# Sending x through DRAM on another queue, with later takes and a longer last part of the down projection

## The chip, the cores and the metric

The kernel runs on one core of one Trainium2 chip. The metric is the device time of one execution in microseconds. TensorE is PE in what follows, VectorE DVE, ScalarE ACT, GpSimd POOL and SyncE SP; PEld is PE's loading of weights.

## The reference

The reference is a decoder trunk of four layers over x, 256 rows of 1024 floats. Each layer is three blocks: a SwiGLU feed-forward (inner width 2816) with half weight, a mixer, and a second SwiGLU. The mixer is a short gated convolution in layers 0 and 3, latent attention in layer 1 and chunked spatial gating in layer 2.

```python
def swiglu(x, w_gate, w_up, w_down):
    return (jax.nn.silu(x @ w_gate) * (x @ w_up)) @ w_down

for i in range(DEPTH):
    x = x + 0.5 * swiglu(rms_norm(x, norm_g[i, 0]), ffn_gate[i, 0], ffn_up[i, 0], ffn_down[i, 0])
    hn = rms_norm(x, norm_g[i, 1])
    x = x + mixer(hn)                     # conv, latent attention or spatial gating, by i % 3
    x = x + 0.5 * swiglu(rms_norm(x, norm_g[i, 2]), ffn_gate[i, 1], ffn_up[i, 1], ffn_down[i, 1])
```

All is float32, and all weights are read once from DRAM.

## The kernel before

x stays in SBUF as two tiles of 128 rows (x0 and x1). Each has its own stream of work, a Python generator; stream 0 is four turns ahead of stream 1, and after that the two take turns. Both use the same weights, each unit of them once.

Weights come in units of 128 x 1024 floats: two k-tiles of 512 columns, or one k-tile of 1024. `W.load` (L91) issues a unit's DMA on SP into one of 6 raw buffers. `W.make` writes whi, the unit rounded for the fast matmul, on ACT (L104), and `W.complete` wlo, the rest, on DVE (L111); there are 9 pairs of these. A raw buffer's next load is issued right behind the wlo that frees it. Activations are split in the same way (L244 on ACT, L245 on DVE), and each product is three matmuls (L290, L291, L293). So one turn of one stream, with one unit, is six matmuls of 128 x 512.

The order on every engine is written out by hand. `later(n, fn)` puts work off by n turns, counted over both streams; `later(1, ..)` runs at the end of the same turn.

A block ends in `rows_into_x`: the first k-tiles go into both column halves of the result, and the last `tail` k-tiles first into half 0 and then into half 1. The end of a half adds it to x (`residual`, L391 after a feed-forward, L389 after a mixer) and calls `prepare_x`, which makes the left operand of the next block: x transposed, scaled by the norm's gain, split in two. Some halves are transposed by PE (`turn_by_pe`, L252 and L430). The others go through DRAM: a transpose within 32 x 32 squares on DVE (L406), a write to DRAM (L411), four reads (L415), and a "take" of four scalings on ACT (L420) and the split (L244, L245). Writes and reads stand on ACT's own DMA queue. X_WRITE, X_READ and X_TAKE say how many turns after the half's end they come. Both halves go through DRAM after a feed-forward, except ahead of the attention, where half 1 goes by PE; after a mixer half 0 goes by PE. Each stream does 17 such round trips, 34 in all.

```python
DOWN_TAIL, OUT_TAIL = 8, 4
X_TURN, X_WRITE, X_READ, X_TAKE = 2, 1, 4, 8
```

DOWN_TAIL is the tail of the down projection (22 k-tiles), OUT_TAIL that of a mixer's last product (8). The square sum of x for the norm (L372) stands on ACT. The feed-forward's hidden tiles go through DRAM too (`turned`), with write (L266) and reads (L270) on SP. While a stream is between blocks, weights are made 3 units ahead, else 4 (`CHAIN_AHEAD`, `AHEAD`).

Of the kernel before, what the change touches and what calls it, by code (L numbers as in the profile page):

```python
# [47 lines left out]
AHEAD = 4  # L48
CHAIN_AHEAD = 3
LAG = 4  # L50
DOWN_TAIL, OUT_TAIL = 8, 4
X_TURN, X_WRITE, X_READ, X_TAKE = 2, 1, 4, 8
IDLE_FIRST, IDLE_DMA, IDLE_PE, IDLE_MLA = 1, 2, 2, 4
SKEW = 2
K_POOL, K_SUM, K_SCALE, K_TURN, Q_ROPE, Q_TURN, Q_SUM, Q_WAIT = 2, 2, 3, 2, 1, 3, 3, 3
# [10 lines left out]
class Weights:  # L66


    def __init__(self, nc, raw_pool, pool):
        self.nc, self.raw_pool, self.pool = nc, raw_pool, pool  # L70
        self.raws = []
        self.units = []
        self.made = []
        self.half_made = []
        self.loaded = []

    def add(self, w, c0, width, n_kt, per_unit, k=0):

        v = w.rearrange("(kt p) n -> p kt n", p=P)
        while k < n_kt:  # L80
            n_rows = min(n_kt - k, per_unit * (1 if len(self.units) < SMALL else max(1, PER_RAW * UNIT // (per_unit * width))))
            for j in range(0, n_rows, per_unit):
                self.units.append((len(self.raws), j, min(per_unit, n_rows - j), width))
            self.raws.append((v[:, k : k + n_rows, c0 : c0 + width], n_rows, width))
            k += n_rows
# [23 lines left out]
    def complete(self):  # L109
        for hi, lo, src, upto in self.half_made:  # L110
            self.nc.vector.tensor_tensor(out=lo, in0=src, in1=hi.bitcast(F32), op=ALU.subtract)  # L111
            self.load(upto)
        self.half_made.clear()

    def get(self, u, ahead):
        for _ in range(2):
            if len(self.made) < min(len(self.units), u + ahead):
                self.make()
        return self.made[u]
# [3 lines left out]
def trunk(ctx: ExitStack, tc: tile.TileContext, x, positions, norm_g, ffn_gate, ffn_up, ffn_down,  # L123
          conv_w_in, conv_k, conv_w_out, mla_w_a, mla_q_norm, mla_w_uq, mla_kv_norm, mla_w_ukv,
          mla_q_gain, mla_k_gain, mla_w_o, sg_w_in, sg_v_norm, sg_w_s, sg_b, sg_w_out, out):
    nc = tc.nc
# [12 lines left out]
    def name(tag):  # L139
        ids[0] += 1  # L140
        return f"{tag}_{ids[0]}"

    def slot(shape, dtype=F32):
        return slots.tile(shape, dtype, tag="s", name=name("s"))
# [20 lines left out]
    def later(turns, fn):  # L165
        ids[0] += 1
        put_off.append((turn[0] + turns, ids[0], fn))
# [8 lines left out]
    W = Weights(nc, raw_pool, w_pool)  # L176
# [64 lines left out]
    def split(src, shape):  # L241

        hi, lo = slot(shape, F32R), slot(shape, F32R)
        nc.scalar.activation(hi, src, AF.Copy)  # L244
        nc.vector.tensor_tensor(out=lo, in0=src, in1=hi.bitcast(F32), op=ALU.subtract)  # L245
        return hi, lo
# [128 lines left out]
    def square_x(t, h):  # L375
        sums_of_x[t][h] = square_sum(x_half(t, h))
# [6 lines left out]
    def x_half(t, h):  # L383
        return xs[t][:, h * 512 : (h + 1) * 512]
# [8 lines left out]
    def gain_at(i, which, h):  # L393
        g0 = (i * 3 + which) * NK + 4 * h
        return columns[0][:, g0 : g0 + 4]

    def prepare_x(t, h, i, which, halves_by_dma):

        g = gain_at(i, which, h)
        lhs[t][h] = None  # L400
        later(1, lambda: square_x(t, h))
        if not halves_by_dma[h]:
            later(X_TURN, lambda: turn_by_pe(t, h, g))
            return
        z = slot([P, 4, 4, 32])
        nc.vector.transpose(z.rearrange("p j k b -> p k j b"), x_half(t, h).rearrange("p (k j b) -> p k j b", j=4, b=32))  # L406
        d = dram.tile([4, 32, 4, 4, 32], F32, tag="xturn", name=name("xturn"))
        y = slot([P, 4, 4, 32])

        def write():  # L410
            nc.scalar.dma_start(out=d.rearrange("i a j k b -> (i a) j k b"), in_=z)  # L411

        def read():
            for j in range(4):
                nc.scalar.dma_start(out=y[32 * j : 32 * j + 32], in_=d[:, :, j].rearrange("i a k b -> a i k b"))  # L415

        def take():
            xg = slot([P, 4, P])
            for k in range(4):
                nc.scalar.activation(xg[:, k, :].rearrange("p (i b) -> p i b", b=32), y[:, :, k], AF.Copy, scale=g[:, k : k + 1])  # L420
            lhs[t][h] = split(xg, [P, 4, P])

        later(X_WRITE, write)
        later(X_READ, read)
        later(X_TAKE, take)

    def turn_by_pe(t, h, g):
        tr = transposed([xs[t][:, (4 * h + k) * P : (4 * h + k + 1) * P] for k in range(4)])
        xg = slot([P, 4, P])
        nc.vector.tensor_tensor(out=xg, in0=tr, op=ALU.mult, in1=g.unsqueeze(2).broadcast_to([P, 4, P]))  # L430
        lhs[t][h] = split(xg, [P, 4, P])
# [593 lines left out]
```

## Time and profile before

| | |
|---|---|
| median of 3 runs | 1918.91 us (1911.62 to 1919.62) |
| the profiled execution's own time | 1915.99 us |
| its span | 1914.3 us |
| PE busy | 1861.1 us, 97% of the span |
| DVE, ACT busy | 1121.0 us, 917.8 us |
| mean granted clock of PE | 0.990 |
| DMA | 209 GB/s over the span |

Busy time of PE is the time in which at least one matmul was under way; matmuls overlap, so the mean of one (385 ns) is longer than the time from one start to the next. Engines that are not busy may still be held: ACT's time at issuing DMAs, and at waiting in its queue for one that has not landed, is not counted as busy.

### The profile page before, as it was taken

To read this page: it belongs to the slowest core of one execution; us is meant where nothing else is said; L and a number is where in the kernel's file an instruction comes from. 1 tells how busy PE (TensorE), PEld (TensorE's weight loads), DVE (VectorE), ACT (ScalarE), POOL (GpSimd) and SP (SyncE) were. 2 spreads that over 40 slices of the span, in tenths; PEclk is the share of its full clock that TensorE was granted. 3 is DMA by queue.
4 is the path that set the end of the run, shared out by engine and by line. 5 is a ranking of instruction groups with operands and counts; after the bars stand their busy time and mean duration, and the time that the engine had idled before them with its cause. 6 is when DMAs were issued, how large, how long until landed. Compare 5 with 4: busy or idle time off the path is not lost.

```text
span 1914.3 us, 23335 instructions
## 1 busy us (share of the span) xinstructions
PE 1861.1 (97%) x8518; PEld 1514.9 (79%) x8518; DVE 1121.0 (59%) x1357; ACT 917.8 (48%) x1300; POOL 104.7 (5%) x222
## 2 busy tenths in 40 slices
PE   9999999999999989999989999999999999999999
PEld 7888777888688868788868887878887887787887
DVE  5564575665566466666456655655646564766562
ACT  5443545443544376544454445454435443545442
POOL 1000000000421031000010000000000000000000
PEclk9999999999999988999999999999999999999999
DMA  7776556776677630677768776567866785566782
GB/s 259 246 234 215 187 180 196 243 240 211 202 247 238 201 118 23 196 239 235 231 188 260 231 234 184 175 204 240 256 204 206 238 263 186 178 195 196 239 252 94
DMA packets 224883, 400.25 MB, mean 209 GB/s; under 512 B 17126, under 2 KB 77696, under 8 KB 224768
## 3 DMA queue, kind: packets, MB, share of 16 engines
q1 hardware_dynamic: 199280, 379.25, 62.9%
q10 hardware_dynamic: 24880, 18.41, 3.2%
q0 software_dynamic: 608, 1.11, 0.3%
q8 instruction: 66, 1.08, 0.2%
q14 instruction: 49, 0.40, 0.1%
HBM read 365.67 MB, written 33.03 MB: 208 GB/s over the span
## 4 chain that ended last, share of the span: by engine, by line
PE 80%; DMA 7%; ACT 6%; DVE 4%; ACTq 2%; issue 1%; DVEq 0%
PE acc L291 26%; PE acc L293 26%; PE acc L290 25%; DMA s<-xturn 4%; DMA xturn<-s 3%; DVE wlo L111 2%; ACT whi L104 2%; ACTq L415 2%; PE tr L252 1%; ACT s L372 1%; ACT s L420 1%; PE acc L927 1%; ACT s L244 1%; PE acc L900 1%; DVE x L391 1%
## 5 line engine op out<-in xcount | busy, mean ns | idle before, releaser
L290 PE MATMUL acc<-whi,s 128*128 128x512 f32 (+1 forms) x2664 | 1032.1, 387 | 15.9 <-ACT whi L104 14.1
L291 PE MATMUL acc<-wlo,s 128*128 128x512 f32 (+1 forms) x2664 | 1026.2, 385 | 17.5 <-DVE wlo L111 17.4
L293 PE MATMUL acc<-whi,s 128*128 128x512 f32 (+1 forms) x2664 | 983.5, 385 | 0.0
L111 DVE TENSOR_TENSOR wlo<-raw,whi 128x1024 fp32r<-128x1024 f32 (+1 forms) x634 | 750.8, 1213 | 250.8 <-ACT whi L104 245.7
L104 ACT ACTIVATE whi<-raw 128x1024 fp32r<-128x1024 f32 (+1 forms) x634 | 639.0, 1048 | 262.3 <-PE acc L293 140.9
L290 PEld LDWEIGHTS acc<-whi,s 128*128 128x128 f32 x2664 | 504.0, 189 | 130.5 <-ACT whi L104 23.5
L291 PEld LDWEIGHTS acc<-wlo,s 128*128 128x128 f32 x2664 | 503.8, 189 | 129.2 <-DVE wlo L111 25.9
L293 PEld LDWEIGHTS acc<-whi,s 128*128 128x128 f32 x2664 | 503.2, 189 | 107.0 <-DVE s L245 2.3
L468 ACT ACTIVATE s<-acc,rstd 128x512 f32<-128x512 f32 (+1 forms) x96 | 62.6, 652 | 434.8 <-PE acc L293 428.8
L476 DVE SCALAR_TENSOR_TENSOR s<-acc,rstd,s 128x512 f32<-128x512 f32 (+1 forms) x96 | 67.6, 704 | 186.1 <-PE acc L293 184.5
L277 DVE TENSOR_TENSOR s<-big,s 128x512 fp32r<-128x512 f32 x96 | 61.7, 643 | 128.0 <-ACT s L276 128.0
L380 POOL TENSOR_TENSOR total<-ss,ss 128x1 f32<-128x1 f32 x26 | 17.3, 664 | 1475.0 <-ACT s L372 1475.0
L245 DVE TENSOR_TENSOR s<-s,s 128x512 fp32r<-128x512 f32 (+1 forms) x58 | 39.5, 681 | 63.6 <-ACT s L244 63.6
L372 ACT ACTIVATE s<-x 128x512 bf16<-128x512 f32 x48 | 30.0, 625 | 90.6 <-DVE x L391 51.5
L276 ACT ACTIVATE s<-big 128x512 fp32r<-128x512 f32 x96 | 56.2, 586 | 27.8 <-DMA big<-turn 27.5
L391 DVE SCALAR_TENSOR_TENSOR x<-acc,x 128x512 f32<-128x512 f32 x32 | 22.0, 688 | 78.6 <-PE acc L293 78.6
L478 DVE STREAM_TRANSPOSE big<-s 128x512 f32<-128x512 f32 (+1 forms) x96 | 64.1, 667 | 3.3
L244 ACT ACTIVATE s<-s 128x512 fp32r<-128x512 f32 (+1 forms) x58 | 36.4, 627 | 41.7 <-DVE s L526 21.6
L420 ACT ACTIVATE s<-s,columns 128x128 f32<-128x128 f32 x136 | 43.2, 388 | 27.5 <-DMA s<-xturn 27.4
L252 PE MATMUL tr<-ident,s 128*128 128x128 f32 (+1 forms) x222 | 34.5, 284 | 8.1 <-DVE s L770 3.3
L252 PEld LDWEIGHTS tr<-ident,s 128*128 128x128 f32 (+1 forms) x222 | 26.7, 141 | 16.0 <-DVE s L770 5.1
L406 DVE STREAM_TRANSPOSE s<-x 128x512 f32<-128x512 f32 x34 | 24.2, 712 | 1.2
(123 smaller groups left out, 414.6 us busy)
## 6 DMA issues: line engine op xcount, KB each, us to landing
raw<-in_ffn_gate_dram SPq DMA_DIRECT2D x176, 512.0 KB, 4.8
raw<-in_ffn_up_dram SPq DMA_DIRECT2D x176, 512.0 KB, 4.8
raw<-in_ffn_down_dram SPq DMA_DIRECT2D x176, 512.0 KB, 4.9
raw<-in_conv_w_in_dram SPq DMA_DIRECT2D x48, 512.0 KB, 4.3
turn<-big SPq DMA_DIRECT2D x32, 512.0 KB, 4.2
big<-turn SPq DMA_DIRECT2D x128, 128.0 KB, 4.1
xturn<-s ACTq DMA_DIRECT2D x34, 256.0 KB, 2.5
s<-xturn ACTq DMA_DIRECT2D x136, 64.0 KB, 3.7
```

Of the source, the lines that this page charges most:

```text
L104: nc.scalar.activation(hi, src, AF.Copy)
L111: self.nc.vector.tensor_tensor(out=lo, in0=src, in1=hi.bitcast(F32), op=ALU.subtract)
L252: nc.tensor.transpose(tr[: part.shape[-1], n, :], part, ident)
L276: nc.scalar.activation(hi.rearrange("p k (i b) -> p k i b", b=32), src, AF.Copy)
L277: nc.vector.tensor_tensor(out=lo.rearrange("p k (i b) -> p k i b", b=32), in0=src, in1=hi.bitcast(F32).rearrange("p k (i b) -> p k i b", b ...
L290: nc.tensor.matmul(ps, lhsT=ah[:, k, :], rhs=wh[:, wk, c], start=first, stop=False)
L291: nc.tensor.matmul(ps, lhsT=ah[:, k, :], rhs=wl[:, wk, c], start=False, stop=False)
L293: nc.tensor.matmul(ps, lhsT=al[:, k, :], rhs=wh[:, wk, c], start=False, stop=last)
L420: nc.scalar.activation(xg[:, k, :].rearrange("p (i b) -> p i b", b=32), y[:, :, k], AF.Copy, scale=g[:, k : k + 1])
L468: nc.scalar.activation(sg[n], ps[:, :w], AF.Silu, scale=r)
L476: nc.vector.scalar_tensor_tensor(out=h, in0=ps[:, :w], scalar=r, in1=sg[n], op0=ALU.mult, op1=ALU.mult)
L478: nc.vector.transpose(z[0][:, :, k0 : k0 + w // P].rearrange("p j k b -> p k j b"), h.rearrange("p (k j b) -> p k j b", j=4, b=32))
```

## The change

Writes and reads of x's round trip are issued by SP instead of ACT. From the write's place to the reads' place no weight load is put into SP's order: `complete` notes what is wanted, and `hold` issues it when no round trip is between the two places. X_READ goes from 4 turns to 3, X_TAKE from 8 to 12, and DOWN_TAIL from 8 k-tiles to 12.

```diff
-DOWN_TAIL, OUT_TAIL = 8, 4
-X_TURN, X_WRITE, X_READ, X_TAKE = 2, 1, 4, 8
+DOWN_TAIL, OUT_TAIL = 12, 4
+X_TURN, X_WRITE, X_READ, X_TAKE = 2, 1, 3, 12
...
     def complete(self):
         for hi, lo, src, upto in self.half_made:
             self.nc.vector.tensor_tensor(out=lo, in0=src, in1=hi.bitcast(F32), op=ALU.subtract)
-            self.load(upto)
+            self.wanted = max(self.wanted, upto)
         self.half_made.clear()
+        self.hold(0)
+
+    def hold(self, by):
+
+        self.held += by
+        if not self.held:
+            self.load(self.wanted)
...
         def write():
-            nc.scalar.dma_start(out=d.rearrange("i a j k b -> (i a) j k b"), in_=z)
+            W.hold(1)
+            nc.sync.dma_start(out=d.rearrange("i a j k b -> (i a) j k b"), in_=z)
 
         def read():
             for j in range(4):
-                nc.scalar.dma_start(out=y[32 * j : 32 * j + 32], in_=d[:, :, j].rearrange("i a k b -> a i k b"))
+                nc.sync.dma_start(out=y[32 * j : 32 * j + 32], in_=d[:, :, j].rearrange("i a k b -> a i k b"))
+            W.hold(-1)
```

The place that the prediction walks through is the change from layer 0's second feed-forward to layer 1's first, about 470 to 514 us in the trace of before. There the old block's last units are 160 to 163 (158 to 163 after the change) and the new block begins with unit 164; acc, whi and raw carry the unit's number.

ACT's order there before. xturn_472 is the write for half 1 of x0; s_488, s_498 are takes.

```order
L411 DMA xturn_472_4014<-s_471_4012 128x512
L415 DMA s_461_3988<-xturn_460_3987 32x4x128 x4
L415 DMA s_473_4015<-xturn_472_4014 32x4x128 x4
L104 ACTIVATE whi167_4052<-raw167_3891 128x1024
L104 ACTIVATE whi168_4070<-raw168_3918 128x1024
L420 ACTIVATE s_488_4079<-s_461_3988,columns0_84 128x128 x4
L244 ACTIVATE s_489_4084<-s_488_4079 128x512
L420 ACTIVATE s_498_4102<-s_473_4015,columns0_84 128x128 x4
L244 ACTIVATE s_499_4107<-s_498_4102 128x512
L372 ACTIVATE s_502_4112,ss_501_4111<-x1_79 128x512
L411 DMA xturn_493_4100<-s_492_4098 128x512
L104 ACTIVATE whi169_4121<-raw169_3936 128x1024
```

ACT's order at the same place after the change.

```order
L381 ACTIVATE s_481_4021,ss_480_4020<-x0_78 128x512
L106 ACTIVATE whi167_4052<-raw167_3904 128x1024
L106 ACTIVATE whi168_4070<-raw168_3922 128x1024
L431 ACTIVATE s_488_4079<-s_461_3952,columns0_84 128x128 x4
L253 ACTIVATE s_489_4084<-s_488_4079 128x512
L381 ACTIVATE s_499_4103,ss_498_4102<-x1_79 128x512
L106 ACTIVATE whi169_4116<-raw169_3940 128x1024
L431 ACTIVATE s_506_4143<-s_473_4019,columns0_84 128x128 x4
L253 ACTIVATE s_507_4148<-s_506_4143 128x512
L106 ACTIVATE whi170_4152<-raw170_3977 128x1024
L106 ACTIVATE whi171_4155<-raw171_3989 128x1024
```

The two rows of eight reads and the writes have left ACT; whi167 stands right behind the square sum, and the take of half 1 of x0 (s_506 now, s_498 before) stands behind whi169 instead of ahead of it.

SP's order there before.

```order
L91 DMA raw168_3918<-in_ffn_gate_dram 128x2x512
L91 DMA raw169_3936<-in_ffn_gate_dram 128x2x512
L91 DMA raw170_3958<-in_ffn_gate_dram 128x2x512
L91 DMA raw171_3976<-in_ffn_gate_dram 128x2x512
L91 DMA raw172_4021<-in_ffn_up_dram 128x2x512
L91 DMA raw173_4062<-in_ffn_up_dram 128x2x512
```

SP's order after the change, with the last three of the four round trips of this place.

```order
L421 DMA xturn_460_3951<-s_459_3949 128x512
L425 DMA s_461_3952<-xturn_460_3951 32x4x128 x4
L93 DMA raw170_3977<-in_ffn_gate_dram 128x2x512
L93 DMA raw171_3989<-in_ffn_gate_dram 128x2x512
L421 DMA xturn_472_4018<-s_471_4016 128x512
L425 DMA s_473_4019<-xturn_472_4018 32x4x128 x4
L93 DMA raw172_4035<-in_ffn_up_dram 128x2x512
L93 DMA raw173_4062<-in_ffn_up_dram 128x2x512
L93 DMA raw174_4089<-in_ffn_gate_dram 128x2x512
L421 DMA xturn_493_4100<-s_492_4098 128x512
L425 DMA s_494_4101<-xturn_493_4100 32x4x128 x4
L93 DMA raw175_4126<-in_ffn_gate_dram 128x2x512
```

Each write stands with its four reads directly behind it, and the loads come in groups of two or three between such pairs.

## Rows read from the trace of the kernel before

**Rows 1.** Waits of PE over the span: total us, times, longest us

```profile
PE acc L291 <- DVE wlo L111: 17.4, 23, 0.8
PE acc L290 <- ACT whi L104: 14.1, 16, 2.0
PE tr L252 <- DVE x L391: 4.7, 2, 3.5
```

**Rows 2.** Windows: length, busy us per engine (x instructions), granted clock, DMA share, GB/s

```profile
187.00:217.00 30.00, 26.87 (x105) 20.32 (x104) 15.08 (x17) 16.02 (x31) 3.00 (x6) 0.94 0.61 182
308.00:318.00 10.00, 7.88 (x27) 5.74 (x26) 4.45 (x5) 6.66 (x10) 0.00 (x0) 0.83 0.61 180
486.00:514.00 28.00, 23.88 (x94) 16.91 (x93) 13.52 (x14) 17.27 (x29) 10.42 (x37) 1.00 0.64 171
668.00:692.00 24.00, 19.32 (x82) 16.62 (x81) 11.62 (x15) 11.18 (x23) 2.05 (x6) 0.86 0.38 113
798.00:806.00 8.00, 5.75 (x24) 4.18 (x23) 2.52 (x3) 4.94 (x9) 0.00 (x0) 1.00 0.54 155
968.00:995.00 27.00, 22.12 (x88) 15.73 (x87) 12.53 (x15) 14.43 (x28) 3.68 (x7) 1.00 0.60 181
1168.00:1187.00 19.00, 15.90 (x57) 11.41 (x56) 8.53 (x9) 11.02 (x21) 1.29 (x3) 0.91 0.55 153
1255.00:1263.00 8.00, 5.88 (x25) 4.24 (x24) 2.60 (x3) 4.01 (x7) 0.00 (x0) 1.00 0.44 121
1434.00:1452.00 18.00, 15.39 (x59) 10.38 (x58) 8.53 (x9) 11.01 (x21) 1.28 (x3) 1.00 0.57 158
1622.00:1642.00 20.00, 16.80 (x65) 11.43 (x64) 8.53 (x9) 12.01 (x23) 1.28 (x3) 1.00 0.56 166
1731.00:1742.00 11.00, 8.84 (x31) 6.50 (x30) 4.88 (x5) 6.65 (x10) 0.00 (x0) 0.84 0.57 172
1500.00:1540.00 40.00, 40.00 (x174) 32.37 (x173) 25.52 (x27) 17.91 (x21) 0.00 (x0) 1.00 0.71 223
```

**Rows 3.** Timeline of ACT, 470 to 490 us: start, us, [idle before <- releaser]

```profile
471.12 0.34 ACTq L411 DMA_DIRECT2D xturn<-s  x1
...
479.97 1.28 ACT L420 ACTIVATE s<-s,columns 128x128 f32<-128x128 f32 x4 [2.93 <-DMA s<-xturn]
...
484.40 5.48 ACTq L415 DMA_DIRECT2D s<-xturn  x8
489.93 1.06 ACT L104 ACTIVATE whi<-raw 128x1024 fp32r<-128x1024 f32 x1 [5.84 <-DMA s<-xturn]
```

**Rows 4.** Timeline of PE, 490 to 493 us

```profile
491.04 0.51 PE L290 MATMUL acc<-whi,s 128*128 128x512 f32 x1 [0.50 <-ACT whi L104]
492.31 0.50 PE L291 MATMUL acc<-wlo,s 128*128 128x512 f32 x1 [0.76 <-DVE wlo L111]
```

**Rows 5.** Timeline of ACT, 294 to 318 us

```profile
309.12 1.88 ACTq L415 DMA_DIRECT2D s<-xturn  x4
311.10 2.95 ACT L104 ACTIVATE whi<-raw 128x1024 fp32r<-128x1024 f32 x3 [5.21 <-DMA s<-xturn]
```

**Rows 6.** Chain that ended last, around 304 us: start, us, what

```profile
304.43 4.67 DMA xturn<-s
```

**Rows 7.** Instructions that touch tile xturn: duration ns min/median/max; the transfers' landing

```profile
L415 ACTq DMA_DIRECT2D s<-xturn x136: 309/444/1943, 184.6 to 1734.1; - x136
...
DMA to landing us min/median/max: 1.8/3.4/6.1
```

**Rows 8.** Instructions that touch tile raw: landing of the weight loads

```profile
DMA to landing us min/median/max: 3.1/4.7/10.0
```

**Rows 9.** Groups by line and shape, 470 to 514 us: busy us, mean ns

```profile
L111 DVE TENSOR_TENSOR wlo<-raw,whi 128x1024 fp32r<-128x1024 f32 x14 | 16.7, 1223 | 13.0 <-ACT whi L104 13.0
L104 ACT ACTIVATE whi<-raw 128x1024 fp32r<-128x1024 f32 x15 | 15.1, 1049 | 12.7 <-issue 6.0 <-DMA s<-xturn 5.8 <-ACT s L372 0.5
...
L391 DVE SCALAR_TENSOR_TENSOR x<-acc,x 128x512 f32<-128x512 f32 x4 | 2.8, 688 | 8.4 <-PE acc L293 8.4
```

**Rows 10.** Waits of SP over the span: total us, times, longest us

```profile
SPq L91 <- DVE wlo L111: 1156.3, 510, 44.7
```

**Rows 11.** The page's DMA issues, the hidden tiles' write: KB each, median us to landing

```profile
turn<-big SPq DMA_DIRECT2D x32, 512.0 KB, 4.2
```

More of the change, by code (lines that the diff above doesn't have):

```diff
@@ L75, in __init__ @@
         self.loaded = []
+        self.held = 0
+        self.wanted = 0
     def add(self, w, c0, width, n_kt, per_unit, k=0):
```

## The prediction

> **What bounds the kernel now.** I read the page first: PE is busy 97% of the span, so the end can only move by time in which PE stands or runs slowly. Then the waits of PE [rows 1]: they name wlo and whi, the split weights, made by DVE and ACT, not a transfer and not x. A weight can be late because its load is late, because its buffer is not free, or because the engine that makes it is held. To tell these apart I looked at the eleven changes from one block to the next: their windows [rows 2] (all but the last row) are 203 us long with PE busy for 168.6, so they hold 34.4 of the 53.2 us in which PE is idle at all (1914.3 - 1861.1).
>
> The same windows price them. In the middle of a block (the last row) PE starts 174 instructions in 40 us, 0.230 us each, with no idle time. In each of the other rows I take the length less 0.230 us times the count: 5.85, 3.79, 6.38, 5.14, 2.48, 6.76, 5.89, 2.25, 4.43, 5.05 and 3.87 us, in the rows' order, 51.9 us in all (the eight shorter transposes of the fourth row count as full, which makes it low). Some of this is the clock: in rows with a granted clock below 1.00 (0.94, 0.83, 0.86, 0.91, 0.84) one minus it, times the length, is 1.8, 1.7, 3.4, 1.7 and 1.8 us, 10.4 us together. There PE ran for some us at 1.2 instead of 2.4 GHz after it had stood. No stand, and this should be gone too.
>
> What holds the weights is seen on ACT [rows 3]. At 484.40 it begins to issue eight reads of x; they wait for x's write, and for eight issues at 0.44 us each [rows 7]. Until 489.93 it does nothing else, and the units whi167 and whi168 stand behind them in its order. PE takes unit 167 at 491.04 and its wlo at 492.31 [rows 4]; ACT and DVE then stay late, and units 169 to 171 are waited for as well. After a mixer it is the same with four reads: ACT is held until 311.10 by a write that took 4.67 us [rows 5, 6]. A second, smaller hold is the take that comes before its reads have landed, 2.93 us at 479.97 [rows 3].
>
> **The change part by part.** I follow the change at 470 us in counts of one turn, six matmuls, 1.38 us. Time 0 is the end of half 0 of x0, now after unit 157.
>
> *DOWN_TAIL.* Half 0 ends after 10 + 6 turns of its stream instead of 14 + 4, so four turns of both streams, 5.5 us, earlier; the half 1 that follows ends where it did. Units of two k-tiles by 512 columns have as many floats as one k-tile by 1024, so matmuls, whi and wlo cost the same: nothing.
>
> *The queue.* ACT loses 34 writes and 136 reads and, above all, the waits behind which weights stood. SP takes them; it stands 1156 us of the span waiting for wlo [rows 10], so the issues cost nothing there. What matters is who is queued behind SP's new waits: weight loads only.
>
> *X_READ and X_TAKE.* Reads follow the write directly, and SP waits for its landing. Takes come four turns later on ACT. Is x still in time? Half 1 of x0 is the tightest. It ends at 12 turns, 16.6 us; residual and transpose on DVE are 1.4 us (0.69 for L391 [rows 9], and as long for the transpose), so the write goes at 18.0. In before, write and reads together took 8.85 us, 471.12 to 479.97 [rows 3]: x is there at 26.8. ACT reaches this take after the square sum of x1's half 1 (ended at 18 turns, 24.8, ready at 26.3) and whi169 (1.05 us [rows 9]), at 27.4; the take ends near 29.3, whi170 at 30.3, wlo170 at 31.5. PE wants unit 170 after 25 turns, at 34.5. So 3 us are to spare. Half 1 of x1 goes out at 26.2 and is wanted by ACT only behind the gate's SiLU near 40; the halves 0 have over 14 us. After a mixer whi104 would be made at 308.3 where PE wants unit 104 at about 310.4: 1 to 2 us to spare, the smallest margin of all.
>
> *The hold.* A load that is held comes later by the write's landing and four issues: at most 6.1 us [rows 7] plus 1.8 us. raw172 goes behind the third round trip, near 18.0 + 4.7 + 1.8 = 24.5 (the write's 4.67 us of [rows 6]), lands 4.7 us later in the median [rows 8] at 29.2, and ACT wants it at 31.4. With the longest landing, 10.0 us, it comes at 34.5; whi and wlo end 2.3 us later, at 36.8, and PE wants unit 172 after 29 turns, at 40. The reserve of weights already made covers it.
>
> A transfer on SP behind weight loads has one precedent here: the hidden tiles' write, twice as large, lands in 4.2 us in the median [rows 11]. x's transfers on ACT's queue land in 1.8 to 6.1 us [rows 7]. I take the same 8.85 us on SP for the round trip as the nearest measured; from below 2 x 1.8 + 1.3 = 4.9 us, from above 2 x 6.1 + 1.3 = 13.5 us (two landings and three more issues). At 4.9 nothing is gained over 8.85, since ACT gets to the take later anyway; at 13.5 the tightest take starts at 31.5, 4 us late, and its unit is 1 to 2 us late at PE.
>
> The Trainium skill (DMA: Bandwidth & Descriptors, Queues, rings and completion order) says that each DMA engine takes turns between the queues for which it has work, and takes what stands within one queue in the order in which it was issued. By it x, which on ACT's queue takes turns with the weights, would on SP's stand behind every load already issued, which speaks against the change; the hold stops new loads but not those. The trace neither shows it nor excludes it: 4.2 us for the larger write fits both. If it decided, x would come at the upper bound above, which is the first rival below.
>
> *The sum.* Ten changes of block lose 51.9 - 5.1 = 46.8 us now. I leave 0.5 us in each for starts of matmuls and small waits: 41.8 back. Ahead of the attention (5.1 us) PE waits for its own transposes behind L391, 3.5 us at worst [rows 1], which a held DVE causes in part; half, 2.5 us. Together 44 us: 1915.99 - 44 = 1872 us for the profiled execution. That one lies 2.9 us below the median of the three runs shown and inside their range; I forecast 1 us above it, 1873 us.
>
> **Rivals.** *ACT goes on waiting, at the takes.* x lands at the upper bound, and each wait moves from the reads to the take, with whi behind it. For: ACT did wait there 2.93 us. Against: four more turns are 5.5 us. About half of the 44 us stays: 1916 - 22 + 1 = 1895 us.
>
> *The loads come late: slower than before.* Four round trips fall into some 31 us, and SP is closed to loads for up to 7.9 us in each. Six raw buffers are 6 x 2.76 = 16.6 us of PE's work; less a landing of 4.7 us, the reserve is 12 us. If two closed stretches run into each other without a load between them, 15.8 us pass, and PE stands. Price: two late loads in each of the six changes with both halves through DRAM, at the 3.8 us between 15.8 and 12, and half a clock for as long again (1.7 us [rows 2]): 12 x 5.5 = 66 us, against 44 gained: 1938 us. It decides where a write has not landed when the next half ends. Against it: SP's order has two or three loads between any two round trips, and DMA share is only 0.55 to 0.64 in these windows [rows 2].
>
> *The lost time is not ACT's.* If PE's waits came from the handover itself (no work for a stream between blocks), the weights would be on time and something else late: 1916 us. Against it: PE's waits name whi and wlo, not x.
>
> **How the numbers follow.** Forecast 0.63, half of it 0.17, no change 0.09, slower 0.11. The forecast's own range is 1862 (all 51.9 us, and a little more ahead of the attention) to 1885 (1 us or so left in each change, and none back ahead of the attention). To leave out no more than 2 in 10 the range goes on over the half case: 1861 to 1902 us. A measurement of this kernel tells about 0.5%, 9.6 us, from no change. Faster by more than that: 0.63 + 0.17 = 0.80; within it 0.09; slower 0.11.
>
> **What would show it.** Right: ACT has no DMA issues of x; the waits of PE for wlo and whi fall from 31.5 us to below 10; the five rows with a low clock show 1.00 but for the attention's; the windows hold one matmul per 0.23 us; SP waits for xturn's landing instead. The take of half 1 shows no wait for its reads, or a short one. Wrong: whi or raw waiting for a weight load's landing at 500 to 515 us (starved), ACT idle ahead of the takes until the reads land (half), or PE idle with whi already made.

## The result and the profile after

The changed kernel takes 1857.3 us in the median of four runs (1856.6 to 1858.79), the kernel before 1916.5 us in four: ratio 0.969, 95% interval 0.967 to 0.972, so 59 us less. The forecast was faster, 1873 us, range 1861 to 1902 us: the direction and the mechanism came out, the size was a quarter too small, and the time lies 4 us below the range.

The first lines of the page of after, and its chain by engine. In the chain of before PE had 80% and DMA 7%.

```profile
span 1854.9 us, 23375 instructions
...
PE 1833.3 (99%) x8518; PEld 1506.0 (81%) x8518; DVE 1119.6 (60%) x1357; ACT 913.9 (49%) x1300; POOL 103.9 (6%) x222
...
PE 96%; ACT 2%; DVE 2%; issue 0%; DMA 0%; DVEq 0%; ACTq 0%
```

PE's longest waits in the trace of after (total us, times, longest us), against [rows 1]:

```profile
PE tr L261 <- DVE s L781: 5.1, 6, 2.2
PE acc L300 <- DVE wlo L113: 2.1, 3, 0.8
...
PE acc L299 <- ACT whi L106: 1.3, 2, 0.8
```

The waits for wlo and whi were 31.5 us and are 3.4 us. The wait for L391 ahead of the attention (4.7 us) is gone from the list. What stands first now lies inside the attention.

Windows of after around eight of the eleven changes of block, the change into the attention being the fourth row, and one window in the middle of a block as the last (columns as in [rows 2]):

```profile
183.00:211.00 28.00, 28.00 (x123) 22.67 (x122) 17.89 (x19) 18.24 (x32) 3.59 (x6) 1.00 0.62 207
301.00:311.00 10.00, 10.00 (x44) 8.08 (x43) 3.35 (x4) 4.99 (x10) 0.00 (x0) 1.00 0.85 288
470.00:496.00 26.00, 26.00 (x114) 21.07 (x113) 14.17 (x16) 15.90 (x29) 14.37 (x49) 1.00 0.72 237
645.00:668.00 23.00, 22.39 (x106) 18.80 (x105) 13.14 (x16) 12.82 (x25) 1.89 (x6) 1.00 0.58 183
772.00:780.00 8.00, 8.00 (x36) 6.51 (x35) 3.93 (x4) 3.16 (x5) 0.00 (x0) 1.00 0.70 230
935.00:960.00 25.00, 25.00 (x110) 20.25 (x109) 17.27 (x19) 18.02 (x32) 4.27 (x7) 1.00 0.67 218
1129.00:1147.00 18.00, 18.00 (x79) 14.51 (x78) 10.34 (x11) 10.37 (x19) 2.11 (x5) 1.00 0.62 199
...
1675.00:1685.00 10.00, 10.00 (x45) 8.10 (x44) 4.63 (x4) 5.10 (x9) 0.00 (x0) 1.00 0.74 255
1455.00:1495.00 40.00, 40.00 (x175) 32.53 (x174) 22.21 (x24) 15.79 (x19) 0.00 (x0) 1.00 0.80 254
```

But for the attention's row PE has no idle time here, and starts 4.4 to 4.5 instructions per us as in the middle of a block; the clock is at its upper level in all of them.

PE's idle time fell from 53.2 us to 21.6 (1854.9 - 1833.3), which is 31.6 of the 59 us. The mean granted clock rose from 0.990 to 0.998: one minus it, times the span, is 19 us before and 4 after, so at most some 15 us more go with the clock, of which the prediction read 10.4 in its windows. This is an estimate, since PE is idle in part of the slow stretches. The rest is time in which PE counts as busy and yet starts fewer matmuls: in the third row of [rows 2], at a clock of 1.00, it is idle for 4.1 us and loses 6.4.

Where the time went is best read by matching PE's instructions: both traces have 8518, and away from the changes of block they stand in the same order, so I subtract the start of each 60th in after from that in before and see where the difference grows.

| change into | grows by, us | forecast |
|---|---|---|
| start of the kernel | 1.0 | none |
| conv, layer 0 | 6.0 | 5.4 |
| feed-forward | 4.2 | 3.3 |
| feed-forward, layer 1 | 6.6 | 5.9 |
| attention, up to its projections | 6.6 | 2.5 |
| within the attention | 1.3 | none |
| feed-forward | 2.8 | 2.0 |
| feed-forward, layer 2 | 7.0 | 6.3 |
| spatial gating | 6.0 | 5.4 |
| feed-forward | 2.6 | 1.8 |
| feed-forward, layer 3 | 4.7 | 3.9 |
| conv, layer 3 | 5.3 | 4.6 |
| feed-forward | 4.1 | 3.4 |
| sum | 58.2 | 44.3 |

No other step of 60 instructions changes it by as much as 0.25 us; the smaller steps bring the difference of the two spans to 59.4 us.

ACT in the stretch that the prediction walked through, in the trace of after (start, us, [idle before <- releaser]). The half's end that was called time 0 is 453.7.

```profile
471.13 0.63 ACT L381 ACTIVATE s<-x 128x512 bf16<-128x512 f32 x1 [1.52 <-DVE x L400]
...
479.45 0.63 ACT L381 ACTIVATE s<-x 128x512 bf16<-128x512 f32 x1 [3.87 <-DVE x L400]
479.99 0.19 ACT L381 ACTIVATION_READ_ACCUMULATOR s<-x 128x1 f32 x1
480.08 1.04 ACT L106 ACTIVATE whi<-raw 128x1024 fp32r<-128x1024 f32 x1
481.03 1.26 ACT L431 ACTIVATE s<-s,columns 128x128 f32<-128x128 f32 x4
482.32 0.63 ACT L253 ACTIVATE s<-s 128x512 fp32r<-128x512 f32 x1
482.86 1.99 ACT L106 ACTIVATE whi<-raw 128x1024 fp32r<-128x1024 f32 x2
```

The tightest take begins at 481.03, 27.3 us after time 0, where the prediction had 27.4, and no wait stands ahead of it. The last of its reads landed at 480.5, half a us earlier. Where ACT stood for DMAs [rows 3] it stands for x's own residual, with nothing behind it that PE lacks.

SP at the same place in after:

```profile
455.17 0.34 SPq L421 DMA_DIRECT2D xturn<-s  x1
457.24 1.75 SPq L425 DMA_DIRECT2D s<-xturn  x4
...
471.87 0.34 SPq L421 DMA_DIRECT2D xturn<-s  x1
476.90 1.93 SPq L425 DMA_DIRECT2D s<-xturn  x4
478.94 1.01 SPq L93 DMA_DIRECT2D raw<-in_ffn_up_dram  x2
480.05 0.41 SPq L93 DMA_DIRECT2D raw<-in_ffn_gate_dram  x1
480.51 0.46 SPq L421 DMA_DIRECT2D xturn<-s  x1
486.52 1.75 SPq L425 DMA_DIRECT2D s<-xturn  x4
```

A write with no load just ahead of it is followed by its reads 2.1 us later, one behind three loads 6.0 us later. In the median of after's page the write now takes 4.2 us to land and a read 2.0 us:

```profile
xturn<-s SPq DMA_DIRECT2D x34, 256.0 KB, 4.2
s<-xturn SPq DMA_DIRECT2D x136, 64.0 KB, 2.0
```

In before's page the same rows are:

```profile
xturn<-s ACTq DMA_DIRECT2D x34, 256.0 KB, 2.5
s<-xturn ACTq DMA_DIRECT2D x136, 64.0 KB, 3.7
```

One is longer by what the other is shorter. From the issue of the write to the landing of the last read a round trip takes 7.8 us in the median of after and 8.2 in before, so faster transfers are not what the change gained. The Trainium skill (DMA: Bandwidth & Descriptors, Queues, rings and completion order) has each DMA engine take one queue's work in the order of issue, and the 6.0 us behind three loads agree with it; it did not decide, because x is not what is waited for. All takes of after together wait 1.7 us for x:

```profile
ACT s L431 <- DMA s<-xturn: 1.7, 2, 1.5
```

### The profile page after: what moved, and what is told of

Its sections match the earlier page's. It is cut to its first block, busy times and chain, and to the rows that moved or that the text cites. A ratio compares the mean times of both kernels' runs of the same rounds, so it can differ in the third digit from the quotient of the medians.

```text
span 1854.9 us, 23375 instructions
## 1 busy us (share of the span) xinstructions
PE 1833.3 (99%) x8518; PEld 1506.0 (81%) x8518; DVE 1119.6 (60%) x1357; ACT 913.9 (49%) x1300; POOL 103.9 (6%) x222
## 4 chain that ended last, share of the span: by engine, by line
PE 96%; ACT 2%; DVE 2%; issue 0%; DMA 0%; DVEq 0%; ACTq 0%
PE acc L299 31%; PE acc L300 31%; PE acc L302 31%; PE tr L261 1%; PE acc L938 1%; PE acc L911 1%; ACT whi L106 1%; DVE wlo L113 0%; DVE s L530 0%; ACT s L836 0%; ACT s L253 0%; PE acc L620 0%; DMA s<-in_norm_g_dram 0%; ACT s L817 0%; ACT s L860 0%
## 5 line engine op out<-in xcount | busy, mean ns | idle before, releaser
L253 ACT ACTIVATE s<-s 128x512 fp32r<-128x512 f32 (+1 forms) x58 | 36.5, 629 | 42.1 <-DVE s L537 21.6
```

## The experiments

Theory A is the prediction's: ACT, held by its own DMA queue, makes the weights late. B says that the take came too early, C that half 0 ended too late; D to G came up on the way. Each kernel was timed beside the kernel before, whose median in the three groups was 1913.9, 1915.1 and 1913.5 us. Traces are matched by PE's instructions as above.

### SP's queue alone

```diff
-            nc.scalar.dma_start(out=d.rearrange("i a j k b -> (i a) j k b"), in_=z)
+            nc.sync.dma_start(out=d.rearrange("i a j k b -> (i a) j k b"), in_=z)
...
-                nc.scalar.dma_start(out=y[32 * j : 32 * j + 32], in_=d[:, :, j].rearrange("i a k b -> a i k b"))
+                nc.sync.dma_start(out=y[32 * j : 32 * j + 32], in_=d[:, :, j].rearrange("i a k b -> a i k b"))
```

> The kernel before with one edit: x's write and reads are issued by SP; times (4 and 8 turns), tail and loads as before. Theory A (ACT held by its own DMA queue is the loss): the eight-read stands of ACT go, the take at 8 turns (11 us) may still wait 1 to 3 us for x; 30 to 45 of the 59 us come back, 1871 to 1887 us. Theory B (the early take is the loss): the take waits as long as the reads did, at most 15 us come back, 1901 us or more. Theory C (half 0 ends too late): almost nothing, 1910 us or more.

1884.6 us, ratio 0.985 (0.983 to 0.986): 29 us less, as A has it, at the low end. ACT's and PE's waits in this trace:

```profile
ACT s L420 <- DMA s<-xturn: 120.3, 28, 9.0
```

```profile
PE acc L290 <- ACT s L244: 9.6, 8, 2.0
PE acc L291 <- DVE wlo L111: 6.9, 11, 1.4
...
PE acc L290 <- ACT whi L104: 0.8, 1, 0.8
```

The weights are late for 7.7 us instead of 31.5; ACT now stands at the takes, for x, and PE waits for x itself (L244), eight times, against once in before. Ahead of the attention almost nothing came back (0.6 us).

### The times alone

```diff
-X_TURN, X_WRITE, X_READ, X_TAKE = 2, 1, 4, 8
+X_TURN, X_WRITE, X_READ, X_TAKE = 2, 1, 3, 12
```

> The kernel before with X_READ, X_TAKE at 3 and 12 turns; writes and reads stay on ACT. Theory A: ACT waits at the reads even a turn earlier, and only the 2 to 3 us takes that came too early go; 0 to 12 us back, 1904 to 1917 us. Theory B: 35 us or more back, below 1882 us. Theory C: no change, 1916 us.

2001.8 us, ratio 1.046 (1.044 to 1.047): 88 us more. No theory had this. PE's first wait over the span, and PE around 510 us:

```profile
PE acc L290 <- ACT s L244: 77.4, 14, 7.8
```

```profile
506.61 0.79 PE L290 MATMUL acc<-whi,s 128*128 128x512 f32 x1 [6.71 <-ACT s L244]
523.29 0.80 PE L290 MATMUL acc<-whi,s 128*128 128x512 f32 x1 [5.67 <-ACT s L244]
```

With a tail of 8 k-tiles the new block begins 12 turns after half 0's end, which is where its take now stands, and on ACT behind half 1's square sum, write and reads. PE stands for x, twice at each of seven changes.

### The tail alone

```diff
-DOWN_TAIL, OUT_TAIL = 8, 4
+DOWN_TAIL, OUT_TAIL = 12, 4
```

> The kernel before with DOWN_TAIL 12. Theory A: half 0 has 5.5 us more, but ACT issues the same reads and stands the same time; where the eight reads stand together today they come apart, so 5 to 15 us back, 1901 to 1911 us. Theory B: no change, 1916 us, since the take keeps its 8 turns. Theory C: 30 us or more, below 1887 us.

1906.2 us, ratio 0.996 (0.994 to 0.997): 8 us less, as A has it. The profiled execution, the fastest of the four, gains 12.7 us in the matched traces: 0.8 at the start, some 4 at the first changes, 5.9 ahead of the attention and 1.3 within it; at later changes as much is lost as won. The weights stay late: PE waits 17.7 us for whi and 12.5 us for wlo.

### The changed kernel without the hold

```diff
-            W.hold(1)
...
-            W.hold(-1)
```

> The changed kernel without the hold: loads go into SP's order between write and reads again. Theory A: x's reads come some turns later, behind loads that wait for wlo; half 0 has spare time, half 1 of x0 had 3 us of it, so 0 to 5 us are lost, 1857 to 1862 us. Rival (the hold is what brings x in time): takes wait for landing by 2 us or more at each change, 10 to 25 us lost, 1867 to 1882 us.

1859.9 us, ratio to before 0.972 (0.970 to 0.973), against 0.969 (0.967 to 0.972) with the hold: the intervals overlap, the medians differ by 2.6 us, the matched traces by 1.0 us behind the kernel's start. The hold is worth 1 to 3 us at most, as A has it. Write and reads land in 2.8 and 2.6 us in the median, and a round trip takes 7.3 us against 7.8 with the hold, so the hold does not bring x sooner.

### The changed kernel with a tail of 8

```diff
-DOWN_TAIL, OUT_TAIL = 12, 4
+DOWN_TAIL, OUT_TAIL = 8, 4
```

> The changed kernel with DOWN_TAIL 8 again. Half 0's take comes 12 turns after its end, which is then the turn in which the new block begins; on ACT it stands behind the square sum of half 1, which waits for the old block's end. Theory D (late takes need the longer tail, and this is what cost 88 us in the run with the times alone): PE stands for the take of half 0 at each of 7 changes and in both streams, 3 to 5 us each, and ACT is no longer held by reads: 40 to 70 us above the changed kernel, 1897 to 1927 us. Rival E (those 88 us came from the late take together with reads on ACT): with SP's queue it stays within 10 us of the changed kernel, 1857 to 1867 us.

1884.5 us, ratio 0.985 (0.984 to 0.987): 27 us above the changed kernel, between the two. PE's first wait:

```profile
PE acc L299 <- ACT s L253: 15.1, 13, 1.6
```

The late take does make PE stand for x, 13 times, but for 1.2 us each and not the 5.5 us of the run with the times alone: most of D's price there came with the reads ahead of the take on ACT. ACT itself does not wait for x at any take here.

### The changed kernel with the take at 8 turns

```diff
-X_TURN, X_WRITE, X_READ, X_TAKE = 2, 1, 3, 12
+X_TURN, X_WRITE, X_READ, X_TAKE = 2, 1, 3, 8
```

> The changed kernel with X_TAKE 8. x takes some 7.5 us from write to the last landing (4.2 + 1.3 + 2.0 in its medians) and the take comes 7 turns, 9.7 us, after the half's end, 8.3 us after the write: ACT waits at the takes by up to 1 us in most of 34. Theory A: PE has wlo in hand for that; 0 to 8 us lost, 1857 to 1865 us. Theory B (the later take is the main part): most of the gain goes, 1885 us or more.

1865.3 us, ratio 0.975 (0.973 to 0.977): 8 us above the changed kernel, the edge of A's range. ACT's wait for x:

```profile
ACT s L431 <- DMA s<-xturn: 91.9, 30, 5.3
```

ACT stands 3 us at a take and not the 1 us expected. In the matched traces PE loses 8.8 us, but 1.7 of them at the kernel's start and 1.9 within the attention, where other pairs of executions differ by 1 us and more too; some 5 us are left for the take in this pair.

### The changed kernel on ACT's queue

```diff
-            nc.sync.dma_start(out=d.rearrange("i a j k b -> (i a) j k b"), in_=z)
+            nc.scalar.dma_start(out=d.rearrange("i a j k b -> (i a) j k b"), in_=z)
...
-                nc.sync.dma_start(out=y[32 * j : 32 * j + 32], in_=d[:, :, j].rearrange("i a k b -> a i k b"))
+                nc.scalar.dma_start(out=y[32 * j : 32 * j + 32], in_=d[:, :, j].rearrange("i a k b -> a i k b"))
```

> The changed kernel with writes and reads on ACT's queue again (hold, times and tail as changed). Theory A: ACT is held from each read to the landing of its write, 2 to 5 us at 34 places, and PE waits for whi and wlo as in the run with the tail alone: 30 to 50 us lost, 1887 to 1907 us. Theories B and C (tail and take do it, the queue does not): within 8 us of the changed kernel, 1865 us or less.

1958.1 us, ratio 1.024 (1.022 to 1.025): 101 us above the changed kernel and 43 us above before. B and C are out; A had the sign and half of the size. PE's first waits here, then ACT's:

```profile
PE acc L299 <- ACT whi L106: 45.7, 13, 4.6
PE acc L300 <- DVE wlo L113: 12.0, 20, 0.9
```

```profile
ACT whi L106 <- DMA s<-xturn: 65.2, 12, 6.7
ACT whi L106 <- issue: 61.9, 28, 4.8
```

```profile
510.18 0.79 PE L299 MATMUL acc<-whi,s 128*128 128x512 f32 x1 [4.39 <-ACT whi L106]
```

With X_READ 3 the reads stand directly behind their write on ACT more often, and the whi behind them is later than before. Of the 101 us about 60 are idle time of PE (81.7 us against 21.6) and, as an estimate, 41 the clock: its mean is 0.977 against 0.998, and one minus it, times the span, is 45 us against 4. What a stand of PE costs is thus not its idle time alone.

### The changed kernel with a hold that is 5 turns longer

```diff
-            W.hold(-1)
...
         later(X_READ, read)
+        later(8, lambda: W.hold(-1))
```

> The changed kernel with loads held 5 turns longer, until 8 turns after the half's end; x's own transfers keep their places. At the changes of block with both halves through DRAM two round trips then follow each other in SP's order with no load between them. The slower rival of the prediction (a reserve of 12 us, the raw buffers alone): some 66 us lost, 1905 to 1925 us. Theory F (the 3 to 4 units already split are a reserve of 8 to 11 us more, and x's reads land sooner with fewer loads in flight): 0 to 8 us lost, 1857 to 1865 us.

1858.6 us, ratio 0.972 (0.970 to 0.974): no loss that can be told. In SP's order two round trips follow each other without a load at the six changes with both halves through DRAM (13.8 to 17.2 us pass there from one load's issue to the next), which is the point from which the slower rival was to decide, and PE's wait for wlo is 1.8 us. So the reserve is larger than the raw buffers' 12 us; that the units already split are the rest (F) fits, but was not measured by itself.

### X_READ alone, X_TAKE alone

```diff
-X_TURN, X_WRITE, X_READ, X_TAKE = 2, 1, 4, 8
+X_TURN, X_WRITE, X_READ, X_TAKE = 2, 1, 3, 8
```

> The kernel before with X_READ 3 alone. At most changes one group of reads moves ahead of one whi on ACT (whi169). Theory D (the 88 us that the times alone cost come from takes that stand too late for the new block's start): at most 20 us lost, 1914 to 1936 us. Rival G (they come from reads directly behind their write, which hold ACT through the landing): 50 us or more lost, above 1964 us.

1953.1 us, ratio 1.021 (1.020 to 1.023), 40 us more. And the other, 2, 1, 4, 12:

> The kernel before with X_TAKE 12 alone. Theory D: the take of half 0 stands behind the last half's square sum, write and reads, PE stands for s (L244) 4 to 7 us at each of 7 changes in both streams, 60 to 90 us lost, 1975 to 2005 us. Rival G: 30 us or less lost, below 1946 us.

1949.8 us, ratio 1.019 (1.017 to 1.021), 36 us more. Neither D nor G alone: the 88 us are about the sum. PE's first waits in the one and in the other:

```profile
PE acc L290 <- ACT whi L104: 44.8, 15, 4.6
```

```profile
PE acc L290 <- ACT s L244: 42.2, 14, 5.3
```

With the read a turn earlier the weights are late, with the take four turns later x is.

### SP's queue and the tail

```diff
-DOWN_TAIL, OUT_TAIL = 8, 4
+DOWN_TAIL, OUT_TAIL = 12, 4
...
-            nc.scalar.dma_start(out=d.rearrange("i a j k b -> (i a) j k b"), in_=z)
+            nc.sync.dma_start(out=d.rearrange("i a j k b -> (i a) j k b"), in_=z)
...
-                nc.scalar.dma_start(out=y[32 * j : 32 * j + 32], in_=d[:, :, j].rearrange("i a k b -> a i k b"))
+                nc.sync.dma_start(out=y[32 * j : 32 * j + 32], in_=d[:, :, j].rearrange("i a k b -> a i k b"))
```

> The kernel before with SP's queue and DOWN_TAIL 12; times 4 and 8, no hold. From the run with SP's queue alone (1884.6 us) the tail should give what it gave alone, 8 to 14 us, mostly ahead of the attention: 1868 to 1878 us. If the tail is worth something only with the later take: 1880 us or more.

1864.3 us, ratio 0.974 (0.973 to 0.976): 49 us less, better than either case. ACT's wait for x in this trace:

```profile
ACT s L420 <- DMA s<-xturn: 113.3, 33, 7.3
```

It is nearly as long as with the queue alone, where PE lost 27 us more against the changed kernel; here it costs 6 to 7. The tail is worth 20 us on SP's queue and 8 on ACT's.

### The changed kernel with X_READ 4

```diff
-X_TURN, X_WRITE, X_READ, X_TAKE = 2, 1, 3, 12
+X_TURN, X_WRITE, X_READ, X_TAKE = 2, 1, 4, 12
```

> The changed kernel with X_READ 4. On SP the reads follow the write directly in both; only the place at which loads are released moves by a turn. Theory A: no change, 1856 to 1861 us. Rival (the earlier read is part of the gain): 5 us or more lost, 1862 us or more.

1857.4 us, ratio 0.971 (0.970 to 0.973): no change. On SP the turn that cost 40 us on ACT is worth nothing. None of these kernels beats the changed one.

## Why the prediction was wrong in size

- *What bounds: right.* PE's waits for whi and wlo were ACT's stands at x's DMAs. The queue back on ACT costs 101 us, the queue alone gives 29 us, and with the tail 49 us.
- *The walk: right.* Write, take and whi170 lie within 0.2 us of the forecast, raw172's issue within 0.7 us (25.2 for 24.5). The round trip of the tightest take is 8.6 us where 8.85 was assumed, and x is there half a us ahead of the take, as forecast. The margin of 1 to 2 us after a mixer held as well: nothing is lost there.
- *The sum, its step "I leave 0.5 us in each": failed.* Nothing was left. The ten changes other than the attention's gave 49.3 us, where the sum had 41.8. Of the 7.5 us, 5.0 are this allowance, for which no row stood, and 2.5 the counts of [rows 2]: a window's count takes in the one or two matmuls that were already under way when it opened (105 in the first row, of which 103 start in it), and in short windows these weigh more than in the 40 us that gave the 0.230 us. Counted in steps from start to start, parts of a step included, at the 0.232 us of the middle of a block, the ten windows of before hold 49.3 us, all of which came back.
- *The sum, its step "half, 2.5 us" ahead of the attention: failed, by 4.1 us.* I named a held DVE as a part of the cause and gave it half, without a row for that share. It was nearly all: DVE was held by the same ACT. In before, DVE around 682 us:

```profile
682.15 0.69 DVE L245 TENSOR_TENSOR s<-s,s 128x512 fp32r<-128x512 f32 x1 [5.03 <-ACT s L244]
682.76 0.68 DVE L391 SCALAR_TENSOR_TENSOR x<-acc,x 128x512 f32<-128x512 f32 x1
```

  The residual that PE's transposes wait for stands behind the split of a take, for which DVE stands 5.03 us. The half's last matmul ends at 678.9, so the residual starts 3.9 us late; PE stands 3.5 us for it, and from 682 to 690 us its granted clock is 0.57. In after, where half 0 ends earlier, the residual follows its half's last matmul at once:

```profile
659.72 0.69 DVE L254 TENSOR_TENSOR s<-s,s 128x512 fp32r<-128x512 f32 x1 [1.39 <-ACT s L253]
660.43 0.69 DVE L400 SCALAR_TENSOR_TENSOR x<-acc,x 128x512 f32<-128x512 f32 x1
```

  The tail alone gave 5.9 us here, the queue alone 0.6. I had costed the tail at nothing but earlier x and had not followed the take onto DVE. The row's 5.1 us were low as well, and not by the eight transposes alone: 35 of its matmuls have 416 columns, start 0.19 us apart at full clock, and count there as 0.23. The 1.3 us within the attention are the clock's and not x's: from 733 to 741 us of before it is 0.57, and 0.79 at the same instructions in after (709 to 717 us).
- *1 us at the start and 1 us above the profile.* The first is a difference between two executions ahead of anything that changed; the second held (after's median is 0.7 us above its profiled execution), but it added to the miss.
- *The parts: named, but not weighed.* The prediction priced the later take and the tail by the walk alone. Undone singly, the queue is worth 101 us, the tail 27, the take 5 to 8, the hold 3 at most and the read nothing, far more than 59 together: the tail and the queue are what makes the take's new place free, and on ACT's queue each of the two times costs some 40 us.
- *Rivals.* ACT waiting at the takes is what the queue alone does (120 us of ACT's time) and what queue and tail still do (113 us). The later take removes it, and with the take at 8 turns on SP's queue it is the tail that has x ready for PE: PE's wait for s is 9.6 us without it and 1.3 with it. Late loads: put to the test with the longer hold, and not seen. Lost time that is not ACT's: refuted.

The range ended at 1861 us because it allowed for all 51.9 us "and a little more"; what the windows' counts missed (2.5 us), the attention (1.5 us above its row, and 1.3 within it), the start (1.0 us) and steps too small for the table (1.2 us) went past it.

## What to carry to other kernels

- A DMA whose data are not ready belongs on a queue whose engine makes nothing that the critical engine needs; the price of having it elsewhere is not its issue time (0.44 us) but what stands behind it in order.
- Where a mechanism is removed whole, sum the whole loss from counts of starts at the steady step, and leave an allowance only if a row shows what it pays for; follow each held result through every engine that takes it in order.
- Numbers that set places in an order belong together: a time that is free in one arrangement cost 36 to 40 us in another, so an edit of several is neither the sum of its parts nor safe to take apart.

## What the runs showed that was not expected

An engine's wait has no price of its own. ACT stood 120 us for x with the queue alone and 113 us with queue and tail, and these kernels differ by 20 us; the changed kernel removed nearly all of that wait and won 7 us more. With the queue back on ACT, ACT stands 127 us ahead of whi (65.2 + 61.9), and that kernel is 43 us slower than before, where ACT stands 114:

```profile
ACT whi L104 <- issue: 57.7, 28, 5.0
ACT whi L104 <- DMA s<-xturn: 56.2, 10, 6.6
```

Landing times of x moved between write and reads: 2.5 and 3.7 us in before, 4.2 and 2.0 in after, 2.8 and 2.6 without the hold. The last two kernels differ by 1 to 3 us.
